# Layer 0 of an S5 + SSD + retention trunk: stages divided and reordered, and a third fp32 u tile

## Chip, cores and metric

One core of one Trainium2 chip runs the whole kernel. The metric is device time in microseconds (us) of one execution; the median of 3 runs stands for a kernel.

## What is computed

The input is x, 512 positions by 1024 features in float32; the output has the same shape. There are two layers and a final RMSNorm. Layer 0, which the change touches, is (from the reference, shortened):

```
p   = rmsnorm(x) @ w_in                       # columns: z (2048) | u (1024) | xbc (1536) | dt (16)
y_a = s5_mixer(u) * silu(z_a)                 # 64 groups of 16 channels, diagonal complex state, GELU, GLU
y_b = ssd_mixer(xbc, dt)                      # conv of 4 taps, 16 heads, 4 chunks of 128 positions
y_b = rmsnorm(y_b * silu(z_b), norm_w, 2 groups)
h   = x + concat(y_a, y_b) @ w_out
```

SSD works by chunk: a decay matrix exp(a_l - a_s) for each head times C B^T gives the part within a chunk; a state carried from chunk to chunk gives the part from before. S5 is written here as products with powers of the state matrix: the input of 8 positions is folded into one state step, the 64 steps are scanned, and the outputs are read back through the same powers. Layer 1 is a retention layer (q, k, v and gate projections, rotary, 4 chunks, 4 heads, group norm, output projection); it is not touched.

## The kernel before

Activations lie transposed in SBUF: features on partitions in tiles of 128, and 512 positions along the free side. A projection makes one 128 x 512 tile of results in one PSUM buffer. There are two forms. The unsplit form (`mm1`, line 202) is 8 fp32 matmuls on the raw weight, each of which the trace shows as two instructions. The split form (`mm3`, line 110) is 24 matmuls on parts in the fp32r type: ScalarE copies the weight to a high part and VectorE subtracts it for the low part (`split_w`, line 100), and the same is done once to the normalised x (`parts`, line 251), which gives `xh` and `xl`. `SPLIT` (line 29) names the z and u tiles that take the split form; u0, u1 and all xbc tiles take the unsplit one. u0 and u1 are run on x before it is normalised, and their results are multiplied by the norm `rbc` when they leave PSUM (line 265), because the norm is not known yet.

Layer 0 is cut into stages with one letter each (dictionary at line 477), and `ORDER` (line 36) writes out the sequence by hand:

- `x` m: one xbc tile and its convolution. `d`, `e`: step sizes and decays. `w`: split of the normalised x. `u` m, `z` m: one projection tile; u goes to DRAM and comes back in another layout, z goes to DRAM.
- `q`: S5 parameters, on VectorE, with a rotation table on GpSimd. `b` j: products O for the outputs (lines 764 to 784, GpSimd), written to DRAM. `k` j: the taps (line 786). `a` j (line 710, `s5_state`): loads U, loads `al` and `b`, makes the products `tm` and `al` from them (lines 726 to 731), runs the S matmuls on them (line 734), then the rotation and scan on VectorE. `c` j (line 802): reads O and the taps back and makes the S5 output y5.
- `s` c (line 351, `ssd`): one SSD chunk, for two head groups: transposes, state update, the decay tile `dec` (loaded from DRAM, Abs and Exp on ScalarE, mask on VectorE, lines 386 to 391), the y matmuls (lines 393 to 399) and their eviction.
- `n` gr (line 442, `ssd_norm`): gate, squares and sums on GpSimd and ScalarE, then the column sums and the root (`rstd`, line 161: matmuls `rsg..ps`, twelve small VectorE instructions, transposes `rsg..pb`), then the split into `ybh` and `ybl`. `o` m: output projection of the SSD half (`ob`), which needs all eight `ybh`/`ybl`. `p` m: S5 output times gate, and its split, which all GLU projections `gl` need.

The program text does not set the queues by itself. A scheduler runs through the program on a timeline of planned times before the run. At each step it takes, for each engine, the instruction of the highest priority whose inputs and buffers are ready on that timeline; priority is the place in the program, apart from weight loads and splits (`rank_w`, `ahead`) and evictions (`rank_e`), which are put forward. The order found so is fixed: on the chip each engine takes its instructions in that order, and so does SP, whose queue issues all transfers.

Buffers come from pools by tag (line 26): `v` has 17 slots (12 are the conv tiles), `m` 20, `p` 5, `f` 8, `s` 4, `g` (decay tiles) 3. PSUM has three tags: `acc` 3, `a` 2, `b` 3.

Of the kernel before, what the change touches and what calls it, by code (L numbers as in the profile page):

```python
# [17 lines left out]
P = 128  # L18
# [7 lines left out]
BUFS = {'x': 16, 'v': 17, 'm': 20, 's': 4, 'p': 5, 'f': 8}  # L26
POOL_P = ((1, 1), (2, 1), (3, 1))
WARM = 11
SPLIT = [f"z{m}" for m in range(16)] + [f"u{m}" for m in range(2, 8)]
SILU_Z = tuple(range(8, 16))  # L30
GELU_P = ()
AX, AZ = 200, 600
KEEP = (2, 3)
POOL_Z = (7,)
VEC_X = ((0, 0), (1, 0), (0, 1), (1, 1))
ORDER = """x8 x10 d0 x9 x11 q0 x0 x1 x2 x3 e0 b0 x4 x5 x6 x7 w0 a0 s0 u2 u3 k0 b1 s1 z0 z1 a1 c0 s2 z2 z3 u4 u5 k1 b2
 s3 z4 z5 a2 c1 z6 z7 n0 n1 u6 u7 k2 b3 a3 c2 o0 o1 z8 z9 z10 z11 k3 o2 o3 c3 z12 z13 z14 z15 o4 o5 p0 p1 p2 p3 o6 o7 p4 p5 p6 p7"""
MAGIC = 12582912.0
LOG2E = 1.4426950408889634
LN2_HI = 0.693359375  # L40
# [7 lines left out]
def trunk_kernel(ctx: ExitStack, tc: tile.TileContext, a: dict, out: bass.AP):  # L48
# [13 lines left out]
    def acc(name):  # L62
        return pp.tile([P, 512], F32, name=name, tag="acc", bufs=3)
# [122 lines left out]
    def layer0():  # L186
# [33 lines left out]
        with rank(-3000000):  # L220
            s5pr = t("m", "s5p", n=192).rearrange("p (i w) -> p i w", w=64)
            sp.dma_start(s5pr, a["s5p"])
            sp.dma_start(lnw, a["lnw"])
            w0 = []
            for k in range(KD):
                sp.dma_start(xs[k], a["xT"][k])
                if k == 0:
                    w0 += [ld_raw(a["w_u"][m], f"u{m}") for m in range(1)]
            w0 += [ld_raw(a["w_u"][m], f"u{m}") for m in range(1, 2)]
            for k in range(KD):  # L230
                q = t("p", f"xq{k}")
                act.activation(q, xs[k], AF.Square)
                act.activation(xs[k], xs[k], AF.Identity, scale=lnw[:, 0, k:k + 1])
                if k:
                    vec.tensor_tensor(sq[0], sq[0], q, op=ALU.add)
                sq.append(q)
            pu = [acc(f"u{m}") for m in range(2)]
            for k in range(KD):
                pe.matmul(pu[0], w0[0][:, k, :], xs[k], start=k == 0, stop=k == KD - 1)
            rstd(sq[:1], D, "rs0", rbc)  # L240
            mm1(pu[1], w0[1], xs)
            for k in range(KD):
                vec.tensor_tensor(xn[k], xs[k], rbc, op=ALU.mult)
        tri = const("tri", [P, P], a["tri"])
# [10 lines left out]
                xh.append(h), xl.append(lo)  # L255

        def s5_in(m):
            ps = proj(a["w_u"][m], f"u{m}") if m > 1 else pu[m]
            with rank_e():
                us = t("p", f"us{m}")  # L260
                ud, sd = us.rearrange("p (t k) -> p t k", t=T5), ps.rearrange("p (k t) -> p t k", t=T5)
                if m > 1:
                    act.activation(ud, sd, AF.Copy)
                else:
                    vec.tensor_tensor(ud, sd, rbc.rearrange("p (k t) -> p t k", t=T5), op=ALU.mult)
                sp.dma_start(u_d[:, m * P:(m + 1) * P, :].rearrange("t c k -> c t k"),
                             us.rearrange("p (t k) -> p t k", t=T5))
# [2 lines left out]
            s5.update(s5_params(s5pr))  # L270
            s5_setup(s5)

        s5_in(0)
        s5_in(1)
        sA = [P, NC4, 16]
        dtn = sv.tile(sA, F32, name="dtn")
        dda = sv.tile(sA, F32, name="dda")
# [60 lines left out]
        def conv(m):  # L338
# [8 lines left out]
            act.activation(g, g, AF.Silu)  # L347
            xbc[m] = g
        prev = [None, None]

        def ssd(c):
            yb, bT, cT = xbc[0:8], xbc[8:10], xbc[10:12]
# [13 lines left out]
            for gr in range(2):  # L366
                hs = slice(8 * gr, 8 * gr + 8)
                xdt = t("v", f"xdt{c}{gr}").rearrange("p (h d) -> p h d", d=64)
                ps_x = aux(f"px{c}{gr}", "b")
                for i in range(4):  # L370
                    pe.transpose(ps_x[:, i * P:(i + 1) * P], xbc[4 * gr + i][:, cs], ident)
                vec.tensor_tensor(xdt, ps_x.rearrange("p (h d) -> p h d", d=64),
                                  dtn[:, c, hs].unsqueeze(2).broadcast_to([P, 8, 64]), op=ALU.mult)
                if c < NC4 - 1:
                    xds = t("v", f"xds{c}{gr}")
                    vec.tensor_tensor(xds.rearrange("p (h d) -> p h d", d=64), ps_x.rearrange("p (h d) -> p h d", d=64),
                                      ds[:, c, hs].unsqueeze(2).broadcast_to([P, 8, 64]), op=ALU.mult)
                    ps_s = aux(f"st{c}{gr}", "b")
                    pe.matmul(ps_s, bn[:, gr, :], xds, start=True, stop=True)
                if c > 0:  # L380
                    ps_o = aux(f"yo{c}{gr}", "b")
                    pe.matmul(ps_o, cT[gr][:, cs], prev[gr], start=True, stop=True)
                    yo = t("v", f"yos{c}{gr}")
                    vec.tensor_tensor(yo.rearrange("p (h d) -> p h d", d=64), ps_o.rearrange("p (h d) -> p h d", d=64),  # L384
                                      ec[:, c, hs].unsqueeze(2).broadcast_to([P, 8, 64]), op=ALU.mult)
                dec = tp.tile([P, 8, P], F32, name=f"dec{c}{gr}", tag="g", bufs=3)
                sp.dma_start(dec, at_d[c, hs, :].partition_broadcast(P))
                for i in range(8):
                    act.activation(dec[:, i, :], dec[:, i, :], AF.Abs, bias=nacs[:, c, 8 * gr + i:8 * gr + i + 1])  # L389
                act.activation(dec, dec, AF.Exp, scale=-1.0)  # L390
                vec.tensor_tensor(dec, dec, cbm[:, gr, :].unsqueeze(1).broadcast_to([P, 8, P]), op=ALU.mult)
                ps_y = aux(f"y{c}{gr}", "b")
                for pr in range(4):
                    if c > 0:
                        pe.matmul(ps_y[:, pr * P:(pr + 1) * P], yo[:, pr * P:(pr + 1) * P], ident, start=True, stop=False)  # L395
                    for hh in range(2):
                        i = 2 * pr + hh
                        pe.matmul(ps_y[64 * hh:64 * hh + 64, pr * P:(pr + 1) * P], xdt[:, i, :], dec[:, i, :],
                                  start=c == 0, stop=True)
                for pr in range(4):  # L400
                    m = 4 * gr + pr
                    vec.scalar_tensor_tensor(yb[m][:, cs], xbc[m][:, cs], chp[:, 0, m:m + 1],
                                             ps_y[:, pr * P:(pr + 1) * P], op0=ALU.mult, op1=ALU.add)
                if c == 0:
                    prev[gr] = t("s", f"prev{gr}")
                    act.activation(prev[gr], ps_s, AF.Copy)
                elif c < NC4 - 1:
                    h_ = prev[gr].rearrange("p (h d) -> p h d", d=64)
                    vec.tensor_tensor(h_, h_, cd[:, c, hs].unsqueeze(2).broadcast_to([P, 8, 64]), op=ALU.mult)
                    vec.tensor_tensor(prev[gr], prev[gr], ps_s, op=ALU.add)  # L410
# [31 lines left out]
        def ssd_norm(gr):  # L442
            yb = xbc[0:8]
            sqs = []
            for i in range(4):
                m = 4 * gr + i
                zt = t("p", f"zb{m}r")
                sp.dma_start(zt, z_d[m])
                if m not in SILU_Z:
                    act.activation(zt, zt, AF.Silu)  # L450
                pool.tensor_tensor(yb[m], yb[m], zt, op=ALU.mult)
                act.activation(zt, yb[m], AF.Square)
                if i:
                    pool.tensor_tensor(sqs[0], sqs[0], zt, op=ALU.add)
                sqs.append(zt)
            rg = t("m", f"rg{gr}")
            rstd(sqs[:1], 512, f"rsg{gr}", rg)
            for i in range(4):
# [8 lines left out]
        def out_b(m):  # L467
            ps = acc(f"ob{m}")
            mm3(ps, ld_w(a["w_o0"][m, 1], f"ob{m}"), ybh, ybl)
            with rank_e():  # L470
                x = t("p", f"hb{m}")
                with after(f"ob{m}"):
# [1 line left out]
                vec.tensor_tensor(x, ps, x, op=ALU.add)  # L474
                sp.dma_start(h_d[m], x)

        stage = dict(a=lambda j: s5_state(s5, u_d, j), b=lambda j: s5_kern(s5, j), c=lambda j: s5_out(s5, j),
                     k=lambda j: s5_taps(s5, j), d=steps, e=decay, q=s5_begin, w=parts, u=s5_in,
                     s=ssd, x=conv, z=gate_in, p=glu_in, n=ssd_norm, o=out_b)
        for o in ORDER.split():  # L480
# [195 lines left out]
    def s5_setup(s5):  # L676
# [28 lines left out]
        y_d = dp.tile([8, P, SEQ], F32, name="y_d")  # L705
        o_d = dp.tile([4, 4, P, SEQ], F32, name="o_d")
        eye, dK = const("eye", [P, 16], a["eye"]), const("dK", [P, 8], a["dK"])
        s5.update(eye=eye, dK=dK, kd=kd, bd=bd, y_d=y_d, o_d=o_d, X={}, U={}, y={}, os={})

    def s5_state(s5, u_d, j):  # L710
        rot = s5["rot"]
        U = f(f"U{j}", [P, 16, NK])
        for tt in range(T5):
            sp.dma_start(U[16 * tt:16 * tt + 16],
                         u_d[tt, 256 * j:256 * j + 256, :].rearrange("(g c) k -> c g k", c=16))
        pss = [aux(f"S{j}{c}") for c in range(2)]
        for par in range(2):
            g0 = 16 * j + 8 * par
            al, b, tm = (f(f"{n}{j}{par}", [P, 2, 8, 2, 32]) for n in ("al", "b", "tm"))
# [9 lines left out]
            for c in range(2):  # L729
                eng.tensor_tensor(al[:, c], al[:, c], b[:, 1 - c], op=ALU.mult)  # L730
            eng.tensor_tensor(al[:, 1], al[:, 1], al[:, 0], op=ALU.subtract)
            for c, Pt in enumerate((tm[:, 0], al[:, 1])):
                for i in range(8):
                    pe.matmul(pss[c][64 * par:64 * par + 64, i * NK:(i + 1) * NK],  # L734
                              Pt[:, i].rearrange("p h f -> p (h f)"), U[:, 8 * par + i, :],
# [22 lines left out]
        for par, c in ((0, 0), (1, 0), (0, 1), (1, 1)):  # L758
            q = slice(64 * par, 64 * par + 64)
            eng = vec if (par, c) in VEC_X else pool  # L760
            eng.tensor_tensor(X[par][64 * c:64 * c + 64], gt[c][q], gi[c][q], op=ALU.add if c else ALU.subtract)
        s5["X"][j], s5["U"][j] = X, U

    def s5_kern(s5, j):
        pws, kd, bd = (s5[k] for k in ("pws", "kd", "bd"))
# [364 lines left out]
```

## Time and profile before

| | us |
|---|---|
| median of 3 runs | 927.87 |
| lowest, highest | 927.17, 930.09 |
| profiled execution, its own time | 926.73 |
| its span, first to last instruction | 925.0 |
| TensorE matmul (PE) busy | 874.0 |
| VectorE (DVE) busy | 549.7 |
| ScalarE (ACT) busy | 360.7 |
| GpSimd (POOL) busy | 227.3 |

Times in the trace count from the first instruction. PE's busy time includes work at the lower clock; the granted clock is given for each stretch, as a share of 2.4 GHz. PE reaches layer 1 (the first `qk` matmul) at 513 us. In a line of the timeline the brackets hold the time for which the engine stood idle before the group, and what ended it.

### The profile page before, as it was taken

To read this page: it belongs to the slowest core of one execution; us is meant where nothing else is said; L and a number is where in the kernel's file an instruction comes from. 1 tells how busy PE (TensorE), PEld (TensorE's weight loads), DVE (VectorE), ACT (ScalarE), POOL (GpSimd) and SP (SyncE) were. 2 spreads that over 40 slices of the span, in tenths; PEclk is the share of its full clock that TensorE was granted. 3 is DMA by queue.
4 is the path that set the end of the run, shared out by engine and by line. 5 is a ranking of instruction groups with operands and counts; after the bars stand their busy time and mean duration, and the time that the engine had idled before them with its cause. 6 is when DMAs were issued, how large, how long until landed. Compare 5 with 4: busy or idle time off the path is not lost.

```text
span 925.0 us, 11531 instructions
## 1 busy us (share of the span) xinstructions
PE 874.0 (94%) x4260; PEld 671.8 (73%) x4260; DVE 549.7 (59%) x986; ACT 360.7 (39%) x572; POOL 227.3 (25%) x193
## 2 busy tenths in 40 slices
PE   8797999899796699999999999999999999999996
PEld 4333457677575578788888888888888888888885
DVE  6969549867768856255444364744643544547445
ACT  4311483425334233353434325345421243254432
POOL 0089701730875380000003121301000303110020
PEclk9898999999797789999999999999999999999998
DMA  7394214775664575683543222222222222222322
GB/s 241 94 225 137 93 46 139 244 206 158 214 213 118 145 204 173 213 297 127 188 143 124 92 91 69 69 92 69 91 91 92 93 91 68 92 69 69 115 69 91
DMA packets 73623, 121.44 MB, mean 131 GB/s; under 512 B 27552, under 2 KB 38112, under 8 KB 73440
## 3 DMA queue, kind: packets, MB, share of 16 engines
q1 hardware_dynamic: 73568, 120.72, 41.3%
q8 instruction: 33, 0.54, 0.3%
q14 instruction: 22, 0.18, 0.1%
HBM read 103.61 MB, written 17.07 MB: 130 GB/s over the span
## 4 chain that ended last, share of the span: by engine, by line
PE 62%; DVE 3%; ACT 1%; DMA 1%; SPq 1%; issue 0%; ACTq 0%; DVEq 0%
PE g L114 3%; PE qk L116 3%; PE qk L115 3%; PE g L115 3%; PE g L116 3%; PE qk L114 3%; PE v L909 3%; PE v L910 3%; PE v L908 3%; PE gl L115 2%; PE gl L116 2%; PE gl L114 2%; PE ob L115 2%; PE oa L116 2%; PE out L115 1%; PE out L116 1%
## 5 line engine op out<-in xcount | busy, mean ns | idle before, releaser
L882 POOL TENSOR_TENSOR rt<-rt,ru 128x512 f32<-128x512 f32 x16 | 27.1, 1717 | 134.6 <-DVE ru L881 134.6
L951 POOL TENSOR_TENSOR os<-os,os 128x512 f32<-128x512 f32 x12 | 15.5, 1289 | 139.9 <-ACT os L949 107.0
L777 POOL TENSOR_TENSOR O<-ct,s5pws 128x512 f32<-128x512 f32 x16 | 22.1, 1384 | 109.9 <-DMA ct<-in_s5c_dram 88.4
L861 POOL TENSOR_TENSOR hs<-hs,hs 128x512 f32<-128x512 f32 x7 | 12.3, 1753 | 88.0 <-ACT hs L859 88.0
L345 DVE SCALAR_TENSOR_TENSOR cva<-xbc,cvw,cva 128x511 f32<-128x511 f32 (+2 forms) x36 | 26.7, 742 | 10.9 <-ACT cva L342 10.6
L881 DVE TENSOR_TENSOR ru<-qk,tab 128x512 f32<-128x512 f32 x16 | 11.0, 685 | 32.5 <-PE qk L116 32.5
L389 ACT ACTIVATE dec<-dec,nacs 128x128 f32<-128x128 f32 x64 | 19.6, 388 | 26.3 <-DMA dec<-at_d 26.3
L781 POOL TENSOR_TENSOR O<-O,ot 128x512 f32<-128x512 f32 x16 | 28.0, 1776 | 0.0
L777 POOL TENSOR_TENSOR ot<-ct,s5pws 128x512 f32<-128x512 f32 x16 | 22.7, 1419 | 0.0
L983 DVE TENSOR_TENSOR h<-h,out 128x512 f32<-128x512 f32 x8 | 5.5, 687 | 25.5 <-PE out L116 25.5
L1044 POOL TENSOR_TENSOR fin<-fin,fnw 128x512 f32<-128x512 f32 x4 | 5.0, 1283 | 60.4 <-ACT fq L1008 60.4
L438 POOL TENSOR_TENSOR za6r<-za6r,y 128x512 f32<-128x512 f32 x1 | 1.7, 1719 | 72.2 <-DMA h_d<-hb 72.2
L727 DVE TENSOR_TENSOR tm<-al,b 128x512 f32<-128x512 f32 x10 | 11.1, 1150 | 13.1 <-DMA b<-in_s5bP_dram 9.2
L347 ACT ACTIVATE cva<-cva 128x512 f32<-128x512 f32 x12 | 7.6, 630 | 27.9 <-DVE cva L345 25.1
L503 DVE TENSOR_TENSOR h<-oa,h 128x512 f32<-128x512 f32 x8 | 5.5, 691 | 19.6 <-PE oa L116 19.6
L509 POOL TENSOR_TENSOR s5rt<-rot,s5lv 128x512 f32<-128x512 f32 (+4 forms) x7 | 5.3, 754 | 44.6 <-DVE s5lv L663 44.4
L119 ACT ACTIVATE rh<-rt 128x512 fp32r<-128x512 f32 (+1 forms) x16 | 9.1, 577 | 16.9 <-POOL rt L882 16.9
L734 PEld LDWEIGHTS S<-U,tm 128*64 128x64 f32 x128 | 9.0, 147 | 9.2 <-issue 4.1
L824 PE MATMUL Y<-T,U 128*64 128x128 f32 x128 | 14.4, 273 | 1.3 <-DMA T<-kd 1.3
L120 DVE TENSOR_TENSOR rl<-rt,rh 128x512 fp32r<-128x512 f32 (+1 forms) x16 | 14.9, 956 | 0.6 <-ACT rh L119 0.2
L395 PE MATMUL y<-ident,yos 128*128 128x128 f32 x48 | 12.5, 346 | 2.6 <-DVE yos L384 2.6
L1039 PE MATMUL om<-wh,yh 128*128 128x512 f32 (+1 forms) x40 | 14.0, 349 | 0.5 <-DVE fin L1006 0.5
(1691 smaller groups left out, 2983.0 us busy)
## 6 DMA issues: line engine op xcount, KB each, us to landing
al<-al_d SPq DMA_DIRECT2D x64, 64.0 KB, 3.5
b<-in_s5bP_dram SPq DMA_DIRECT2D x8, 512.0 KB, 3.7
o_d<-O SPq DMA_DIRECT2D x16, 256.0 KB, 3.0
dec<-at_d SPq DMA_DIRECT2D x8, 512.0 KB, 5.2
T<-kd SPq DMA_DIRECT2D x64, 64.0 KB, 2.4
Or<-o_d SPq DMA_DIRECT2D x16, 256.0 KB, 5.5
x<-in_xT_dram SPq DMA_DIRECT2D x8, 256.0 KB, 5.0
u_d<-us SPq DMA_DIRECT2D x8, 256.0 KB, 3.1
```

The lines of the kernel that those rows point to most:

```text
L114: pe.matmul(ps, wh[:, k, :], xh[k], start=start and i == 0, stop=False)
L115: pe.matmul(ps, wh[:, k, :], xl[k], start=False, stop=False)
L116: pe.matmul(ps, wl[:, k, :], xh[k], start=False, stop=stop and i == len(ks) - 1)
L345: vec.scalar_tensor_tensor(g[:, d:], ps[:, 0:SEQ - d], cvw[:, m, j:j + 1], g[:, d:], op0=ALU.mult, op1=ALU.add)
L389: act.activation(dec[:, i, :], dec[:, i, :], AF.Abs, bias=nacs[:, c, 8 * gr + i:8 * gr + i + 1])
L777: pool.tensor_tensor(x.rearrange("p (g k c) -> p g k c", g=4, c=16), ct[:, c, par, 4 * hf:4 * hf + 4].unsqueeze(2).broadcast_to(sh), pws[: ...
L781: pool.tensor_tensor(o, o, tm, op=ALU.add)
L882: pool.tensor_tensor(t1, t1, t2, op=op)
L908: pe.matmul(ps[c], hh[kk][:, cs], wh[:, i, :], start=kk == 0, stop=False)
L909: pe.matmul(ps[c], hh[kk][:, cs], wl[:, i, :], start=False, stop=False)
L910: pe.matmul(ps[c], hl[kk][:, cs], wh[:, i, :], start=False, stop=kk == KD - 1)
L951: pool.tensor_tensor(sqs[0], sqs[0], sx, op=ALU.add)
```

## The change

1. Three u tiles instead of two take the unsplit form ahead of the norm. 2. S5's stage `a` becomes `l` (load U), `g` (load `al`, `b` and make the products) and `a` (S matmuls and scan). 3. SSD's stage `s` ends with the masked decay tile and the state update; `t` does the y matmuls and their eviction. 4. `n` ends with the sum of squares; `r` does the root, the norm and the split. 5. `ORDER` is rewritten. No instruction is added or taken away apart from the third u tile's form.

```
-SPLIT = [f"z{m}" for m in range(16)] + [f"u{m}" for m in range(2, 8)]
+SPLIT = [f"z{m}" for m in range(16)] + [f"u{m}" for m in range(3, 8)]
-ORDER = """x8 x10 d0 x9 x11 q0 x0 x1 x2 x3 e0 b0 x4 x5 x6 x7 w0 a0 s0 u2 u3 k0 b1 s1 z0 z1 a1 c0 s2 z2 z3 u4 u5 k1 b2
- s3 z4 z5 a2 c1 z6 z7 n0 n1 u6 u7 k2 b3 a3 c2 o0 o1 z8 z9 z10 z11 k3 o2 o3 c3 z12 z13 z14 z15 o4 o5 p0 p1 p2 p3 o6 o7 p4 p5 p6 p7"""
+ORDER = """x8 x10 d0 x9 x11 q0 x0 b0 x1 x2 l0 g0 x3 e0 x4 k0 x5 b1 x6 a0 x7 w0 g1 s0 u3 l1 t0 s1 z0 a1 k1 b2 z1 t1 s2 u4 c0 u5
+ t2 l2 g2 s3 z2 a2 k2 b3 z3 t3 u6 c1 u7 z4 l3 g3 z5 n0 z6 a3 z7 c2 n1 z8 k3 r0 z9 z10 r1 c3 z11 o0 p0 p1 o1 z12 p2 z13 p3 o2 z14
+ p4 p5 z15 o3 p6 p7 o4 o5 o6 o7"""
...
-            w0 += [ld_raw(a["w_u"][m], f"u{m}") for m in range(1, 2)]
+            w0 += [ld_raw(a["w_u"][m], f"u{m}") for m in range(1, 3)]
-            pu = [acc(f"u{m}") for m in range(2)]
+            pu = [acc(f"u{m}") if m < 2 else aux(f"u{m}", "b") for m in range(3)]
...
             mm1(pu[1], w0[1], xs)
+            mm1(pu[2], w0[2], xs)
...
-                if m > 1:
+                if m > 2:
                     act.activation(ud, sd, AF.Copy)
...
                 vec.tensor_tensor(dec, dec, cbm[:, gr, :].unsqueeze(1).broadcast_to([P, 8, P]), op=ALU.mult)
+                held[c, gr] = xdt, dec, yo if c > 0 else None
+                if c == 0:
+                    prev[gr] = t("s", f"prev{gr}")
+                    act.activation(prev[gr], ps_s, AF.Copy)
...
+        def ssd_y(c):
+            yb, cs = xbc[0:8], slice(c * P, (c + 1) * P)
+            for gr in range(2):
+                xdt, dec, yo = held[c, gr]
                 ps_y = aux(f"y{c}{gr}", "b")
...
                 sqs.append(zt)
+            held["sq", gr] = sqs
+
+        def ssd_parts(gr):
+            yb, sqs = xbc[0:8], held["sq", gr]
             rg = t("m", f"rg{gr}")
             rstd(sqs[:1], 512, f"rsg{gr}", rg)
...
+    def s5_load(s5, u_d, j):
         U = f(f"U{j}", [P, 16, NK])
...
+    def s5_state(s5, j):
+        s5["P"][j] = []
...
-            for c, Pt in enumerate((tm[:, 0], al[:, 1])):
+            s5["P"][j].append((tm[:, 0], al[:, 1]))
+
+    def s5_scan(s5, j):
+        rot, U = s5["rot"], s5["U"][j]
+        pss = [aux(f"S{j}{c}") for c in range(2)]
+        for par in range(2):
+            for c, Pt in enumerate(s5["P"][j][par]):
```

## Rows read from the trace of the kernel before

**Rows 1.** The page: the span, and each engine's busy time.
```profile
span 925.0 us, 11531 instructions
...
PE 874.0 (94%) x4260; PEld 671.8 (73%) x4260; DVE 549.7 (59%) x986; ACT 360.7 (39%) x572; POOL 227.3 (25%) x193
```

**Rows 2.** Busy time by stretch of the span (the header names the columns).
```profile
core 0: us, PE busy (x) PEld busy (x) DVE busy (x) ACT busy (x) POOL busy (x), PEclk, DMA share, GB/s
23.00:39.50 16.50, 11.32 (x24) 4.78 (x23) 16.50 (x67) 4.41 (x8) 0.00 (x0) 0.79 0.34 96
74.00:98.00 24.00, 18.36 (x38) 7.80 (x37) 23.06 (x32) 5.43 (x8) 23.16 (x26) 0.86 0.26 87
...
172.00:186.00 14.00, 10.22 (x57) 7.28 (x56) 12.53 (x13) 4.93 (x11) 6.28 (x4) 0.88 0.90 294
186.00:240.00 54.00, 54.00 (x364) 40.92 (x363) 32.80 (x54) 24.03 (x49) 13.27 (x11) 1.00 0.65 189
240.00:260.00 20.00, 14.95 (x79) 10.85 (x78) 18.47 (x19) 2.20 (x4) 20.00 (x12) 0.66 0.62 190
260.00:288.00 28.00, 28.00 (x218) 22.23 (x217) 21.48 (x27) 13.77 (x23) 18.62 (x14) 1.00 0.55 182
288.00:332.00 44.00, 26.83 (x144) 21.21 (x143) 33.24 (x57) 14.65 (x24) 22.48 (x16) 0.69 0.50 132
```

**Rows 3.** Timeline of PE to 98 us (start, length, instruction, idle before).
```profile
22.07 1.88 PE L204 MATMUL u<-x,u1w 128*128 128x512 f32 x4
26.92 0.62 PE L171 MATMUL rs0pb<-ident,rs0y 128*128 128x128 f32 x4 [2.97 <-DVE rs0y L158]
29.75 9.90 PE L204 MATMUL xbc<-xn,xbc8w 128*128 128x512 f32 x16 [2.21 <-DVE xn L243]
39.48 7.03 PE L204 MATMUL xbc<-xn,xbc10w 128*128 128x512 f32 x16
...
87.79 9.88 PE L204 MATMUL xbc<-xn,xbc2w 128*128 128x512 f32 x16 [3.43 <-issue]
```

**Rows 4.** Timeline of PE from 170 to 330 us: its longest waits.
```profile
177.18 0.50 PE L116 MATMUL z<-xh,z3l 128*128 128x512 f32 x1 [3.78 <-DVE z3l L107]
...
243.49 1.51 PE L734 MATMUL S<-U,tm 128*64 128x64 f32 x12 [2.42 <-DVE tm L728]
247.64 0.80 PE L395 MATMUL y<-ident,yos 128*128 128x128 f32 x2 [2.64 <-DVE yos L384]
...
295.03 1.84 PE L165 MATMUL rsg0ps<-ones,zb0r 128*128 128x1 f32 x8 [6.16 <-POOL zb4r L454]
299.39 0.87 PE L171 MATMUL rsg0pb<-ident,rsg0y 128*128 128x128 f32 x3 [2.53 <-DVE rsg0y L158]
...
314.47 1.12 PE L734 MATMUL S<-U,tm 128*64 128x64 f32 x16 [1.28 <-ACT ks L796]
...
320.92 1.94 PE L734 MATMUL S<-U,al 128*64 128x64 f32 x16 [3.84 <-DVE al L731]
```

**Rows 5.** Timeline: split u2's first matmul, u3's first; u results times rbc; u2's low part.
```profile
138.43 0.48 PE L114 MATMUL u<-xh,u2h 128*128 128x512 f32 x1
...
143.98 0.39 PE L114 MATMUL u<-xh,u3h 128*128 128x512 f32 x1
...
33.83 2.05 DVE L265 TENSOR_TENSOR us<-u,rbc 128x512 f32<-128x512 f32 x2
...
L107 DVE TENSOR_TENSOR u2l<-u2w,u2h x1: 1224/1224/1224, 118.2 to 118.2; 128x1024 fp32r<-128x1024 f32 x1
```

**Rows 6.** Instructions of line 107, min/median/max ns, and group of z7l in 240 to 332 us.
```profile
L107 DVE TENSOR_TENSOR z11l<-z11w,z11h x1: 1225/1225/1225, 345.2 to 345.2; 128x1024 fp32r<-128x1024 f32 x1
...
L107 DVE TENSOR_TENSOR z7l<-z7w,z7h 128x1024 fp32r<-128x1024 f32 x1 | 2.1, 2115 | 0.0
```

**Rows 7.** Timeline: SP's al loads, DVE's wait at a product; ACT's wait for decay loads.
```profile
57.15 3.19 SPq L722 DMA_DIRECT2D al<-al_d  x6
...
66.17 2.55 DVE L727 TENSOR_TENSOR tm<-al,b 128x512 f32<-128x512 f32 x2 [7.22 <-DMA b<-in_s5bP_dram]
...
ACT dec L389 <- DMA dec<-at_d: 26.3, 6, 7.9
```

More of the change, by code (lines that the diff above doesn't have):

```diff
@@ L257, in s5_in @@
         def s5_in(m):
-            ps = proj(a["w_u"][m], f"u{m}") if m > 1 else pu[m]
+            ps = proj(a["w_u"][m], f"u{m}") if m > 2 else pu[m]
             with rank_e():
@@ L271, in s5_begin @@
             s5_setup(s5)
-        s5_in(0)
-        s5_in(1)
+        for m in range(3):
+            s5_in(m)
         sA = [P, NC4, 16]
@@ L349, in layer0 @@
         prev = [None, None]
+        held = {}
         def ssd(c):
@@ L391, in ssd @@
                 vec.tensor_tensor(dec, dec, cbm[:, gr, :].unsqueeze(1).broadcast_to([P, 8, P]), op=ALU.mult)
+                held[c, gr] = xdt, dec, yo if c > 0 else None
+                if c == 0:
+                    prev[gr] = t("s", f"prev{gr}")
+                    act.activation(prev[gr], ps_s, AF.Copy)
+                elif c < NC4 - 1:
+                    h_ = prev[gr].rearrange("p (h d) -> p h d", d=64)
+                    vec.tensor_tensor(h_, h_, cd[:, c, hs].unsqueeze(2).broadcast_to([P, 8, 64]), op=ALU.mult)
+                    vec.tensor_tensor(prev[gr], prev[gr], ps_s, op=ALU.add)
+        def ssd_y(c):
+            yb, cs = xbc[0:8], slice(c * P, (c + 1) * P)
+            for gr in range(2):
+                xdt, dec, yo = held[c, gr]
                 ps_y = aux(f"y{c}{gr}", "b")
@@ L403, in ssd @@
                                              ps_y[:, pr * P:(pr + 1) * P], op0=ALU.mult, op1=ALU.add)
[L404 to L410, printed above, removed]
         z_d = dp.tile([16, P, SEQ], F32, name="z_d")
@@ L475, in out_b @@
                 sp.dma_start(h_d[m], x)
-        stage = dict(a=lambda j: s5_state(s5, u_d, j), b=lambda j: s5_kern(s5, j), c=lambda j: s5_out(s5, j),
+        stage = dict(l=lambda j: s5_load(s5, u_d, j), g=lambda j: s5_state(s5, j), a=lambda j: s5_scan(s5, j), t=ssd_y, r=ssd_parts, b=lambda j: s5_kern(s5, j), c=lambda j: s5_out(s5, j),
                      k=lambda j: s5_taps(s5, j), d=steps, e=decay, q=s5_begin, w=parts, u=s5_in,
@@ L707, in s5_setup @@
         eye, dK = const("eye", [P, 16], a["eye"]), const("dK", [P, 8], a["dK"])
-        s5.update(eye=eye, dK=dK, kd=kd, bd=bd, y_d=y_d, o_d=o_d, X={}, U={}, y={}, os={})
-    def s5_state(s5, u_d, j):
-        rot = s5["rot"]
+        s5.update(eye=eye, dK=dK, kd=kd, bd=bd, y_d=y_d, o_d=o_d, X={}, U={}, y={}, os={}, P={})
+    def s5_load(s5, u_d, j):
         U = f(f"U{j}", [P, 16, NK])
@@ L715, in s5_state @@
                          u_d[tt, 256 * j:256 * j + 256, :].rearrange("(g c) k -> c g k", c=16))
-        pss = [aux(f"S{j}{c}") for c in range(2)]
+        s5["U"][j] = U
+    def s5_state(s5, j):
+        s5["P"][j] = []
         for par in range(2):
@@ L761, in s5_state @@
             eng.tensor_tensor(X[par][64 * c:64 * c + 64], gt[c][q], gi[c][q], op=ALU.add if c else ALU.subtract)
-        s5["X"][j], s5["U"][j] = X, U
+        s5["X"][j] = X
     def s5_kern(s5, j):
```

## The prediction

> **What bounds the kernel now.** I read the page first, then the busy time stretch by stretch, then TensorE's timeline for its waits, then the instructions that the waits name. The page says that TensorE (PE) is busy in 874.0 of 925.0 us [rows 1], so nothing but PE work and PE waits can set the end. The stretches show where the 51 us without work lie. From 186 to 240 us and from 260 to 288 us PE is busy throughout at a granted clock of 1.00 [rows 2]. The losses sit in five places, all in layer 0: A 23 to 39.5, B 74 to 98, C 172 to 186, D 240 to 260, E 288 to 332 us. In each the granted clock is also below 1.00 (0.66 in D, 0.69 in E), that is, for a part of it PE ran at 1.2 instead of 2.4 GHz after it had waited. The reader is to see that a wait is paid twice: as idle time and as slow work behind it.
>
> What a stretch loses is bounded from its row. Idle time is its length less PE busy. Slow clock costs at most (1 - clock) x length, when all of the slow time fell on work, and half of the idle time less than that, when PE idled only at the slow clock. D: 20.00 - 14.95 = 5.05 idle, 0.34 x 20 = 6.8. E: 44.00 - 26.83 = 17.17 idle, 0.31 x 44 = 13.6. D and E together: 22.2 idle, 20.4 clock, so a loss of 31.5 to 42.7, middle 37 us, or 1.67 us for each us of idle. C: 3.8 idle + 1.7 clock = 5.5 at most.
>
> Who ends the waits: in A the norm chain on VectorE (DVE) [rows 3]; in D and E the S5 products (S waits for tm and al, 2.42 and 3.84), the S matmul behind ks 1.28, the group norm (rsg0ps waits 6.16 for GpSimd's (POOL's) zb4r, rsg0pb 2.53 for DVE), and y behind yos 2.64 [rows 4]. Each waiting instruction is the head of PE's queue, and projections stand behind it.
>
> **The third unsplit u tile.** u2 becomes 16 fp32 matmuls on the unnormalised x, issued while the norm is computed. u0 and u1 end at 23.95 (22.07 + 1.88); then PE waits 2.97 and 2.21, and xbc8's 16 matmuls take 9.90 at the slow clock where xbc10's take 7.03 [rows 3]. With u2, 7.03 long, xbc8 starts near 31.0 and, if the clock holds, ends near 38.0 instead of 39.5: the tile costs nothing, because the norm chain hides it. Without that cover it would cost 7.03. Its later form, 24 split matmuls from 138.43 to 143.98, disappears: -5.5 us [rows 5]. The 1.5 us won at 38 I drop: at 77 to 88 us PE waits for DVE's work anyway (B, DVE busy 23.06 of 24.00 [rows 2]), and DVE gets 1.0 more there (us for u2 with rbc, 2.05 for two) against 1.2 less later (u2l) [rows 5]. So A and B give -5.5, with bounds of -7.0 (kept) and 0 (the hole shrinks and the DVE backlog grows by as much). u2's 512 KB weight now goes ahead of xbc8's on SP's queue; xbc8 is needed only at 31 us.
>
> **The S5 products apart.** Loads of U (8 transfers), then al and b with the products (18 transfers), now come stages ahead of the S matmuls: g0 ahead of x3 and a0 after x6; between g1, g2, g3 and their a there is at least one projection and an SSD or norm stage. Instructions and bytes are the same. SP issues six al loads in 3.19 us [rows 7], so 26 of them hold its queue 13.8 us, ahead of weights for xbc3 and later, which PE reaches from 97.7 (87.79 + 9.88 [rows 3]). DVE once stood 7.22 us at such a product because b had not landed, with conv work queued behind it [rows 7]; that is half of B's cause. Moving g0 earlier could shrink this wait or lengthen it; I take zero, bounds -7 to +7. On POOL the O products b1 to b3 come a little earlier, ahead of the group norm's multiplications instead of partly behind; I price that in the new waits. In D and E the S waits, 2.42 + 1.28 + 3.84, should go, since a projection of 5.5 us or more is queued in their place; what is late next is the scan on DVE, which PE meets only at the Y matmuls.
>
> **The norm's root apart.** n0 and n1 only multiply, square and add; the column sums, the root and the split come as r0 and r1, with two or more projections or S5 stages between. The 6.16 and 2.53 go. Late next: o0 needs all eight ybh and ybl, with c3 and z11 as cover.
>
> Sum for D and E: 7.5 + 8.7 = 16.2 of 22.2 idle us, 0.73 of a loss of 31.5 to 42.7, is 23 to 31; I take the middle, -27. C stays: z3l is late on DVE, 3.78 us [rows 4], and no edit reaches that.
>
> **The SSD outputs apart.** s_c ends with the decay tile and the state update; t_c, with two projections between (one at t0), runs y. xdt and yos of both head groups are held till then (four of the five free v slots beside the 12 conv tiles), and two of the three decay buffers. The trace does not show this. At best it removes the yos wait (2.64, 4.4 with its clock share). At worst the decay loads, for which ScalarE (ACT) now waits 26.3 us out of PE's sight [rows 7], reach PE: 26.3 x 1.67 = 44. I take two new waits of the size of yos's, 2 x 2.64 x 1.67 = +8.8, nearer to the row that PE showed than to ACT's.
>
> **Sum:** -5.5 - 27 + 8.8 = -23.7. The profiled execution took 926.73 us (span 925.0), which is 1.1 below the median of 927.87. 926.7 - 23.7 + 1.1 = **904 us**.
>
> **Rivals.** *DVE takes over.* In the quiet a weight split took DVE 1.22 us (z11l), beside POOL 2.12 (z7l) [rows 6]; in 240 to 332 us DVE is busy 73.2 of 92. If the products and y stay late because DVE is full, only the rsg waits go: 8.69 of 22.2, 14.5 us, less the 8.8: 926.7 - 5.5 - 5.7 + 1.1 = 917. For it: D, where DVE is busy 18.47 of 20. Against: 260 to 288, where DVE is busy 77% with POOL at 66% and PE never waits. The Trainium skill (SBUF — State Buffer, SBUF: two separate sides) says that a DVE instruction with two SBUF inputs and a GpSimd one lock each other out for the whole instruction. By that rule packing the same DVE and POOL work into less time gains nothing from overlap; z7l against z11l agrees with it.
>
> *All waits go.* C, D and E wholly (5.5 + 37) and 7.0 in A: 926.7 - 49.5 + 1.1 = 878. Against: PE's order is fixed before the run, DVE's times vary by the factor above.
>
> *The edit hardly changes the queue.* The scheduler lets ready work pass work that isn't, so u6 and u7, written after n0, already run before it. If the emitted order stays, only u2 counts: 926.7 - 5.5 + 1.1 = 922.
>
> *Slower: the decay tiles.* t_c gives the decay buffers and v slots back late, so the next chunk's load starts late, its Abs, Exp and mask end late, and PE stands at y of t1 to t3 with projections queued behind. The chain then delays n and r, so their waits stay. Gains 5.5 + (7.54 / 22.2) x 37 = 18; cost 26.3 x 1.67 = 44 in full, 22 if half reaches PE: 932 to 954, I say 943. It decides once 0.41 of the 26.3 reach PE. Against: each t has two projections (11 us) as cover, and y waited on DVE, never on a transfer. The Trainium skill (Perfetto Trace Analysis, Optimization Strategy) reads a repeating gap on the engine that should be full as possibly too few buffers; no gap at y repeats in this trace yet.
>
> **Chances.** Forecast 904: 0.42. DVE takes over 917: 0.22. All waits go 878: 0.07. Queue unchanged 922: 0.08. Slower 943: 0.21. Within 0.3% (2.8 us, about what a measurement can tell from no change) fall 0.03 of the fourth and 0.02 of the last. So faster 0.76, same 0.05, slower 0.19. The range runs from 880 (all but the last of the waits) to 938 (the lower half of the slow case); above it lies about 0.12, below about 0.06. The forecast's own range is 890 to 914, by the loss bounds and by none to twice the new waits.
>
> **What would show it.** Right: PE goes from u0/u1 into u2 without a wait and xbc8 takes about 7 us; no wait of PE on zb4r, tm or al; the granted clock of the 90 us ahead of the first ob near 0.95; layer 1, untouched, of the same length. Wrong: PE waits at y with dec behind it; DVE waits for b or al while conv is queued; POOL's O products standing ahead of the norm's multiplications; or ob and gl waiting for ybl and y5l after the last z has been used up as filler.

## The result and the profile after

The changed kernel takes 932.74 us (median of 20 runs, 927.74 to 937.63); the kernel before, run beside it, 927.25 (20 runs, 924.59 to 931.70). The ratio is 1.0054 [1.0036, 1.0072]: slower by 0.5%, where 904 had been forecast. The profiled execution took 927.74 us, the fastest of the 20, so its rows show about 5 us less than the median.

The page of the kernel after, in the part that answers to [rows 1]:

```profile
span 925.9 us, 11510 instructions
...
PE 876.2 (95%) x4252; PEld 670.6 (72%) x4252; DVE 553.2 (60%) x986; ACT 357.8 (39%) x569; POOL 226.2 (24%) x193
```

PE is busy 2.2 us longer than before; the third tile alone takes 7.03 us in its unsplit form (16 matmuls) where its split form took 5.5 (24). Where the time went is seen in six stretches of layer 0, first of the kernel before, then of the kernel after (columns as in [rows 2]):

```profile
0.00:100.00 100.00, 85.64 (x206) 37.76 (x207) 83.39 (x276) 30.32 (x49) 50.89 (x76) 0.93 0.56 161
100.00:160.00 60.00, 60.00 (x292) 36.77 (x291) 38.11 (x60) 36.49 (x67) 10.87 (x11) 1.00 0.32 103
160.00:230.00 70.00, 66.22 (x446) 50.05 (x445) 52.37 (x77) 29.70 (x58) 26.67 (x18) 0.98 0.67 200
230.00:300.00 70.00, 56.26 (x351) 43.60 (x351) 51.84 (x63) 28.19 (x47) 49.63 (x32) 0.84 0.59 182
300.00:390.00 90.00, 79.42 (x496) 62.71 (x496) 50.38 (x70) 27.34 (x40) 27.62 (x18) 0.90 0.60 179
390.00:480.00 90.00, 90.00 (x419) 74.59 (x416) 42.77 (x52) 39.37 (x53) 1.72 (x1) 1.00 0.56 194
```

```profile
0.00:100.00 100.00, 81.53 (x199) 35.67 (x200) 92.16 (x267) 27.46 (x44) 60.58 (x82) 0.95 0.62 179
100.00:160.00 60.00, 57.00 (x240) 30.04 (x239) 38.29 (x58) 33.37 (x59) 25.58 (x22) 0.96 0.29 95
160.00:230.00 70.00, 65.98 (x422) 50.61 (x421) 52.42 (x77) 24.46 (x50) 18.51 (x12) 0.89 0.69 191
230.00:300.00 70.00, 64.65 (x432) 48.28 (x431) 48.19 (x70) 26.28 (x47) 28.80 (x18) 0.95 0.61 167
300.00:390.00 90.00, 79.59 (x505) 64.52 (x504) 53.58 (x84) 46.10 (x74) 30.66 (x20) 0.92 0.64 203
390.00:480.00 90.00, 90.00 (x399) 74.33 (x398) 36.80 (x44) 29.61 (x37) 2.04 (x1) 1.00 0.51 173
```

From 230 to 300 us, where the S5 and norm waits stood, PE gained 8.4 us of work (64.65 for 56.26) and clock (0.95 for 0.84). The first 160 us lost nearly as much, 4.1 and 3.0 us of work, and from 160 to 230 us the clock fell from 0.98 to 0.89. Layer 1 kept its length (411.7 us from the first `qk` matmul to the end in both), so everything was decided here; the output tile ob4 starts at 404.8 us, before at 403.9.

The start, which answers to [rows 3] (timeline of PE in the kernel after):

```profile
13.25 4.46 PE L205 MATMUL u<-x,u2w 128*128 128x512 f32 x10
17.54 1.02 PE L240 MATMUL u<-x,u0w 128*128 128x512 f32 x2
18.40 1.02 PE L205 MATMUL u<-x,u2w 128*128 128x512 f32 x2
...
24.41 0.95 PE L166 MATMUL rs0ps<-ones,xq 128*128 128x1 f32 x8
...
33.13 0.62 PE L172 MATMUL rs0pb<-ident,rs0y 128*128 128x128 f32 x4 [2.52 <-DVE s5scr L665]
35.37 8.82 PE L205 MATMUL xbc<-xn,xbc8w 128*128 128x512 f32 x16 [1.62 <-DVE xn L245]
...
71.98 3.75 PE L205 MATMUL xbc<-xn,xbc11w 128*128 128x512 f32 x4 [6.89 <-issue]
...
99.52 8.80 PE L205 MATMUL xbc<-xn,xbc2w 128*128 128x512 f32 x16 [4.12 <-issue]
```

Twelve of u2's sixteen matmuls (4.46 + 1.02 us) stand ahead of the norm's column sums rs0ps, which start at 24.41 instead of 19.46: u2 has u1's old place, and eight of u1's matmuls and the last four of u0's now stand ahead of rs0ps as well. The waits behind them, 2.52 and 1.62, are still there, and xbc8 starts at 35.37 instead of 29.75. The tile went in front of the hole and moved it. By xbc2 the delay is 11.7 us (99.52 against 87.79). The 6.89 at xbc11 has no releaser in the profile; by time it ends when VectorE's convolution L347 does (71.88), behind work on the S5 parameters.

The sums of squares that rs0ps reads were not late. VectorE's last addition (timeline of DVE, kernel after) ends at 14.27, in the kernel before at 14.47:

```profile
13.58 0.69 DVE L236 TENSOR_TENSOR xq<-xq,xq 128x512 f32<-128x512 f32 x1
```

So rs0ps stood 10 us behind other matmuls in PE's fixed order, and 5 us in the kernel before. No run puts it ahead of u1 too.

The longest waits after that, which answer to [rows 4] (timeline of PE, kernel after):

```profile
157.13 0.50 PE L116 MATMUL u<-xl,u3h 128*128 128x512 f32 x1 [2.32 <-DVE xl L121]
...
213.46 0.80 PE L411 MATMUL y<-ident,yos 128*128 128x128 f32 x2 [4.01 <-DVE yos L387]
...
278.72 0.66 PE L844 MATMUL Y<-Or,X 128*64 128x128 f32 x2 [5.35 <-DMA Or<-o_d]
...
339.33 1.05 PE L166 MATMUL rsg0ps<-ones,zb0r 128*128 128x1 f32 x8
345.04 1.09 PE L172 MATMUL rsg0pb<-ident,rsg0y 128*128 128x128 f32 x4 [4.65 <-DVE rsg0y L159]
```

The S waits and the 6.16 us on zb4r are gone. New are xl 2.32, Or 5.35 and later 2.30; yos grew from 2.64 to 4.01 and rsg0pb from 2.53 to 4.65.

### The profile page after: what moved, and what is told of

Read it like the earlier page. It is cut to its first block, busy times and chain, and to the rows that moved or that the text cites. A ratio compares the mean times of both kernels' runs of the same rounds, so it can differ in the third digit from the quotient of the medians.

```text
span 925.9 us, 11510 instructions
## 1 busy us (share of the span) xinstructions
PE 876.2 (95%) x4252; PEld 670.6 (72%) x4252; DVE 553.2 (60%) x986; ACT 357.8 (39%) x569; POOL 226.2 (24%) x193
## 4 chain that ended last, share of the span: by engine, by line
PE 76%; DVE 7%; DMA 6%; ACT 4%; issue 3%; SPq 2%; POOL 2%; ACTq 0%; POOLq 0%
PE xbc L205 7%; PE g L115 3%; PE qk L117 3%; PE g L116 3%; PE qk L116 3%; PE g L117 3%; PE qk L115 3%; PE v L930 3%; PE v L931 3%; PE v L929 3%; PE z L117 2%; PE z L115 2%; PE z L116 2%; PE gl L115 2%; PE gl L116 2%
## 5 line engine op out<-in xcount | busy, mean ns | idle before, releaser
L347 DVE SCALAR_TENSOR_TENSOR cva<-xbc,cvw,cva 128x511 f32<-128x511 f32 (+2 forms) x36 | 26.7, 741 | 12.3 <-ACT cva L344 11.9
L392 ACT ACTIVATE dec<-dec,nacs 128x128 f32<-128x128 f32 x64 | 19.4, 389 | 16.6 <-DMA dec<-at_d 16.6
L802 POOL TENSOR_TENSOR O<-O,ot 128x512 f32<-128x512 f32 x16 | 21.6, 1379 | 0.0
L844 PE MATMUL Y<-Or,X 128*64 128x128 f32 x64 | 13.6, 297 | 8.1 <-DMA Or<-o_d 8.1
L845 PE MATMUL Y<-T,U 128*64 128x128 f32 x128 | 16.7, 290 | 0.0
L487 DVE TENSOR_TENSOR hb<-ob,hb 128x512 f32<-128x512 f32 x8 | 5.5, 690 | 17.8 <-PE ob L117 17.8
L205 PE MATMUL xbc<-xn,xbc11w 128*128 128x512 f32 x16 | 9.2, 727 | 6.9 <-issue 6.9
L120 ACT ACTIVATE rh<-rt 128x512 fp32r<-128x512 f32 (+1 forms) x16 | 9.1, 577 | 16.9 <-POOL rt L903 16.9
L411 PEld LDWEIGHTS y<-ident,yos 128*128 128x128 f32 x48 | 8.1, 209 | 9.2 <-issue 4.5
```

The lines of the kernel that those rows point to most:

```text
L205: pe.matmul(ps, raw[:, k, :], x[k], start=k == 0, stop=k == KD - 1)
L347: vec.scalar_tensor_tensor(g[:, d:], ps[:, 0:SEQ - d], cvw[:, m, j:j + 1], g[:, d:], op0=ALU.mult, op1=ALU.add)
L802: pool.tensor_tensor(o, o, tm, op=ALU.add)
```

## The experiments

Each median is compared with runs of the kernel before on the same chip; in brackets is the 95% interval of the ratio.

| run | edit | us | ratio to before, 95% |
|---|---|---|---|
| e1 | third u tile alone, old sequence | 949.63 | 1.0234 [1.0195, 1.0273] |
| e2 | change, u2 left split | 934.40 | 1.0082 [1.0052, 1.0111] |
| e3 | stages divided, old sequence, u2 split | 926.48 | 0.9993 [0.9975, 1.0012] |
| e4 | change, u2 behind the column sums | 917.48 | 0.9896 [0.9863, 0.9930] |
| e5 | before, u2 as in e4 | 926.99 | 1.0004 [0.9976, 1.0032] |
| e6 | e4, w0 ahead of a0 | 912.20 | 0.9847 [0.9822, 0.9872] |
| e7 | e4, c1 ahead of k2 and b3 | 914.77 | 0.9873 [0.9842, 0.9903] |
| e8 | e4, r0 and r1 earlier | 920.59 | 0.9929 [0.9901, 0.9956] |
| e9 | e6, norm root in PSUM tag b | 910.55 | 0.9840 [0.9808, 0.9871] |
| e10 | e9, c1 first | 913.70 | 0.9871 [0.9842, 0.9899] |
| e11 | e6, t joined to s | 914.32 | 0.9874 [0.9852, 0.9897] |
| e12 | e6, l and g joined to a | 922.35 | 0.9959 [0.9940, 0.9977] |
| e13 | e2, w0 ahead of a0 | 931.80 | 1.0068 [1.0042, 1.0094] |
| e14 | e9, z written from ScalarE's queue | 909.91 | 0.9826 [0.9801, 0.9851] |

**The change in its parts: e1, e2, e3.** e1 puts the third tile into the kernel before, e2 takes it out of the change, e3 divides the stages but leaves the parts together.

```
 e1:-SPLIT = ... for m in range(2, 8)]    +SPLIT = ... for m in range(3, 8)]  (and u2 out of ORDER)
 e2:-... range(3, 8)]                     +... range(2, 8)]      ORDER: s0 u2 u3 l1 t0
 e3: ORDER = "... w0 l0 g0 a0 s0 t0 u2 u3 k0 b1 s1 t1 z0 z1 l1 g1 a1 c0 ... n0 r0 n1 r1 u6 u7 ..."
```

> Only the third unsplit u tile, in the kernel before. Theory E (the early part loses: u2's matmuls stand ahead of the norm's column sums, so everything behind the norm starts 5 to 6 us later, and the split u2's 5.5 us that go are eaten by that): 926 to 931 us, rs0ps at about 24.4 us instead of 19.5, xbc8 at about 35 instead of 29.75. Theory L (the early part gains the 5.5 of the prediction, the late part loses it again in new waits): about 922 us.

> The change without the third unsplit u tile (u2 split, just ahead of u3). Theory E: 5 us or more faster than the change, 922 to 928 us, with rs0ps back at 19.5 us. Theory L: 5 us slower than the change, about 938 us, since a gain is taken away and the new waits stay.

> The stages divided as in the change, but each part right behind the other in the old sequence, and u2 split as before. If dividing alone costs nothing, 925 to 930 us, as before. If the held tiles or the moved state update cost something by themselves, 932 us or more, with PE waiting at y behind dec.

Dividing costs nothing (926.48). The tile in the old sequence costs 22.4 us, the sequence without it 7.2; the two together cost 5.5. So they are not terms that add. Both theories missed e1 (949.63) and e2 (934.40). Theory E's signs came (rs0ps at 24.54 and xbc8 at 35.50 in e1, rs0ps at 19.19 in e2), but its times left out that xbc2 would start 15.8 us late in e1 (103.62), and that the new sequence loses by itself.

**The tile behind the column sums: e4, e5.** u2's matmuls with the first four feature tiles are queued behind rs0ps, the other four behind rs0pb, and u2's weight is loaded after u1's. The two parts of the edit have no runs of their own.

```
+                sums[name] = pe.matmul(ps[:, c:c + 1], ...).ins
...
+            w0 += [ld_raw(a["w_u"][m], f"u{m}", ahead=-8 * (m - 1)) for m in range(1, 3)]
...
-            mm1(pu[2], w0[2], xs)
+            for k in range(KD):
+                with tc.issue_after(sums["rs0"] if k < 4 else sums["rs0b"]):
+                    pe.matmul(pu[2], w0[2][:, k, :], xs[k], start=k == 0, stop=k == KD - 1)
```

> The change with u2's matmuls queued behind the norm's column sums, the last four behind the norm's transposes, and u2's weight loaded behind u1's. Theory E: rs0ps at about 19.5 us, xbc8 from 31 to 32 us at full clock, and 6 to 11 us faster than the change: 922 to 927 us. Theory L: as the change, within 3 us (930 to 936), since the lead is lost at the next wait on VectorE.

> The kernel before (old sequence, undivided stages) with the third unsplit u tile queued behind the norm's sums, as in e4. If the tile is worth the prediction's 5.5 us once it stands behind the norm, 920 to 923 us, and the new sequence is then worth 3 to 6 us more (e4 has 917.5). If the new sequence brings nothing, this run is at 915 to 919 us; if the tile helps only together with the new sequence, at 926 us or more.

Timeline of PE in e4, the same stretch as above:

```profile
18.90 0.95 PE L168 MATMUL rs0ps<-ones,xq 128*128 128x1 f32 x8
...
23.23 3.60 PE L247 MATMUL u<-x,u2w 128*128 128x512 f32 x8
26.66 0.60 PE L174 MATMUL rs0pb<-ident,rs0y 128*128 128x128 f32 x4
27.10 3.60 PE L247 MATMUL u<-x,u2w 128*128 128x512 f32 x8
30.53 7.03 PE L207 MATMUL xbc<-xn,xbc8w 128*128 128x512 f32 x16
...
86.12 4.56 PE L207 MATMUL xbc<-xn,xbc2w 128*128 128x512 f32 x5 [6.29 <-issue]
```

This is the picture of the prediction: both waits are gone, and xbc8 runs from 30.5 to 37.6 at 7.03. In the new sequence that is worth 15.3 us (932.74 to 917.48), in the old one 22.6 (949.63 to 926.99); the 15.3 is more than theory E's 6 to 11. But in the old sequence the tile so placed gains nothing over the split form: what it saves is waited for later (from 60 us on PE waits 40.1 us in e5, 34.5 before; timeline of PE in e5: xbc2 for 6.68 us, where [rows 3] show 3.43, then a low part of a weight and one of y):

```profile
86.49 3.74 PE L206 MATMUL xbc<-xn,xbc2w 128*128 128x512 f32 x4 [6.68 <-issue]
...
244.26 0.80 PE L116 MATMUL z<-xh,z7l 128*128 128x512 f32 x1 [5.34 <-DVE z7l L107]
...
324.68 0.80 PE L115 MATMUL ob<-ybl,ob0h 128*128 128x512 f32 x1 [7.28 <-DVE ybl L120]
```

**The new waits of the sequence: e6, e7, e8.** Each moves one stage in e4's sequence.

```
 e6:-b1 x6 a0 x7 w0 g1           +b1 x6 x7 w0 a0 g1
 e7:-a2 k2 b3 z3 t3 u6 c1 u7     +a2 c1 k2 b3 z3 t3 u6 u7
 e8:-n1 z8 k3 r0 z9 z10 r1 c3    +r0 n1 z8 r1 z9 k3 z10 c3
```

> e4 with the split of the normalised x (w0) ahead of the first S5 scan (a0) instead of behind it. If the scan's VectorE work holds up xl, PE's waits on xl and z0l near 145 us (2.8 us in e4) go and the time falls by 3 to 8 us, to 910 to 914. If VectorE is full there whatever comes first, 916 to 919.

> e4 with the S5 output stage c1 ahead of the taps k2 and the products b3. If SP's queue is what holds c1's loads of O (they stand behind the write of k2's taps, which waits for VectorE), PE's wait on Or near 264 us (5.6 us) goes and the time falls by 6 to 10 us, to 908 to 912. If the loads are late for lack of slots, the wait stays and so does the time, within 3 us.

> e4 with r0 right behind c2 and r1 right behind z8, so that z8 to z11 and c3 stand between the roots and o0. If the norm chain costs because the projections meant as its cover were used up ahead of it, PE's waits on rsg0pb, ybh and ybl (4.3 us) go and the time falls by 5 to 10 us, to 908 to 913. If the sums of squares on GpSimd come no earlier, PE waits for zb0r or zb4r instead and the time stays or rises.

With w0 first the waits on xl and z0l (1.92 and 0.83 in e4) are gone and 5.3 us with them. With c1 first the Or wait at 264 us is gone, but the time is only 2.7 us lower, which the intervals do not tell apart from e4, and not the 6 to 10 expected; another Or wait, at 347 us, is 4.93 (e4: 1.24).

What held Or at 264 us? SP's own waits in e4 between 236 and 268 us show two things: the write of the taps ks waits for DVE ahead of the Or loads, and one of the Or loads (L832) waits for DVE itself.

```profile
SPq L825 <- DVE ks L823: 13.8, 1, 13.8
SPq L832 <- DVE mg L786: 6.9, 1, 6.9
```

The second ends last (timelines of SP, DVE and PE in e4):

```profile
252.05 1.86 SPq L832 DMA_DIRECT2D Or<-o_d  x2
...
260.22 0.69 DVE L786 TENSOR_TENSOR mg<-X,gi 64x512 f32<-64x512 f32 x1
260.94 0.32 SPq L832 DMA_DIRECT2D Or<-o_d  x1
...
264.02 0.66 PE L848 MATMUL Y<-Or,X 128*64 128x128 f32 x2 [5.59 <-DMA Or<-o_d]
```

Once ks is written, two loads go out by 253.9; the third follows only when DVE has ended a step of a2's scan (260.91), lands 3.0 us later, and PE starts. In the program Or takes its tiles from tag m, as the scan's gi, X and mg do, so this load waits for a buffer. The rival of e7, lack of slots, is thus not refuted but borne out for this wait: with c1 ahead of k2 and b3 its loads also come to their buffers earlier, and e7 cannot tell the two causes apart. The kernel after shows the same ahead of its 5.35 (SP waits 7.0 us for DVE's mg).

e8 missed: rsg0ps stayed at 327.9 us (e4: 328.6), and the time rose by 3.1, within the intervals. The place in the program was not what held the norm's column sums.

**What holds the norm's root: e9, e10.** In the kernel after, POOL's last sum for the first group and the column sums that use it are 20 us apart (timeline of POOL; PE's lines stand above):

```profile
316.89 2.27 POOL L463 TENSOR_TENSOR zb0r<-zb0r,zb3r 128x512 f32<-128x512 f32 x1
```

It ends at 319.16; rsg0ps runs at 339.33, directly ahead of rsg0pb, which then waits 4.65 us for the twelve small DVE instructions. The root's PSUM buffers have tag a, two buffers that the S, K, Y and Yt results use too; e9 gives them tag b.

```
-    def rstd(sqs, n, name, bc):
-        ps = aux(name + "ps")
+    def rstd(sqs, n, name, bc, tag="a"):
+        ps = aux(name + "ps", tag)
...
-            rstd(sqs[:1], 512, f"rsg{gr}", rg)
+            rstd(sqs[:1], 512, f"rsg{gr}", rg, "b")
```

> e6 with the group norm's column sums and transposes in the PSUM tag b (three buffers, free once the SSD stages are done) instead of a (two buffers, which the S, K and Y stages hold). If r0 stood late in PE's queue because the scheduler had no buffer of tag a for it, its sums now come tens of matmuls earlier with projections between sums, transposes and ob: PE's waits on rsg0pb, ybh and ybl (6.2 us in e6) and the slow clock behind them go, and the time falls by 6 to 12 us from 912.2, to 900 to 906. If the sums on GpSimd were the reason, PE waits for zb0r instead and the time stays within 3 us.

> e9 with c1 ahead of k2 and b3 as in e7: the sum of what helped. If the effects add, 2 to 3 us below e9 (e7 gained 2.7 on e4), 898 to 904; if the wait only moves to the next stage on SP's queue, as e9 within 3 us.

Timeline of PE in e9:

```profile
298.25 0.95 PE L168 MATMUL rsg0ps<-ones,zb0r 128*128 128x1 f32 x8
...
312.98 0.65 PE L174 MATMUL rsg0pb<-ident,rsg0y 128*128 128x128 f32 x4 [1.98 <-DVE rsg0y L159]
...
331.56 0.40 PE L848 MATMUL Y<-Or,X 128*64 128x128 f32 x2 [4.63 <-DMA Or<-o_d]
```

The buffer was what held it: POOL's last sum ends at 295.78 in e6 and 295.99 in e9, and the column sums run at 319.95 and 298.25; work stands between them and rsg0pb, and the next waits at `ob` shrink from 0.72 and 0.78 in e6 to 0.41. The time fell by 1.65 us only, less than the intervals can tell apart (0.6 by the ratios): at Or PE waits 4.63 where e6 has 2.74, and at yos 6.53 (195 us) where e6 has 3.25. e10 missed too: c1 first is 3.2 us above e9, as little told apart as the gain in e7; the Or waits stayed (3.00, 1.96, 1.16), and al made PE wait 3.88.

**What the two other divisions are worth: e11, e12.** Both join parts again in e6's sequence.

```
 e11:-s0 u3 l1 t0 s1 z0 a1 k1 b2 z1 t1    +s0 t0 u3 l1 s1 t1 z0 a1 k1 b2 z1   (t2, t3 likewise)
 e12:-x2 l0 g0 x3 ... w0 a0 g1            +x2 x3 ... w0 l0 g0 a0              (1 to 3 likewise)
```

> e6 with each t right behind its s, so that the SSD outputs are no longer apart. If keeping them apart gives y its cover, PE waits more at yos and the time rises by 3 us or more, to 915 or above. If the held xdt, yos and decay tiles cost as much as the cover gives, within 3 us of 912.2; if they cost more, below 909.

> e6 with l and g right ahead of their a, so that the S5 products are no longer apart. If moving them ahead removes PE's waits at the S matmuls, those waits (7.5 us in the kernel before) come back and the time rises by 5 us or more, to 917 or above. If the scheduler pulls the products forward by itself, within 3 us of 912.2.

The S5 products apart are worth 10.1 us. Joined, PE's waits at the S matmuls are 9.6 us in all; e6 keeps 4.7, of which 2.51 behind ScalarE's y and 1.9 without a named releaser. Two of those in e12 (timeline of PE):

```profile
184.63 0.90 PE L759 MATMUL S<-U,tm 128*64 128x64 f32 x6 [2.80 <-POOL tm L747]
...
320.62 1.63 PE L759 MATMUL S<-U,al 128*64 128x64 f32 x16 [4.18 <-POOL al L750]
```

The SSD outputs apart are worth 2.1 us, with overlapping intervals: the wait on yos is 3.62 joined and 3.25 apart. No run joins r to n again, so the third division has no price of its own.

**What stayed open, tried once more: e13, e14.** e13 asks whether xl behind a0's scan is why the sequence without the tile loses; e14 whether SP's queue is why Or is late in e9.

```
 e13 (in e2):-b1 x6 a0 x7 w0 g1               +b1 x6 x7 w0 a0 g1
 e14 (in e9):-sp.dma_start(z_d[m], zt)        +act.dma_start(z_d[m], zt)
```

> The change with u2 kept in its split form (934.40) and w0, the split of the normalised x, moved ahead of a0's scan. Theory: without the third tile the new sequence loses because u2's split matmuls, the first to need xl, stand at 144.5 and 147.4 us for 3.26 and 1.85 us while DVE does a0's scan, and the wait costs 1.67 us for each us. With w0 first these waits go: 934.4 - 8.5 = 926, no slower than before (within 2). Rival: the xl waits are paid for elsewhere (st behind xds 5.81 at 201 us, Or 2.40), the sequence itself is the worse one: 931 or more.

> The best version so far (910.55) with the z results written to DRAM from ScalarE's own queue instead of SyncE's; TensorE's and VectorE's instructions stay in the same order. Theory: the Or loads come late (PE waits 4.63, 1.02 and 1.23 us at 331 to 344) because they stand on SyncE's queue behind a z write that waits 7.1 us for ScalarE; on ScalarE's queue that write holds up no loads, the Or waits fall below 2 us and the time to 905 to 908. Rival: Or is late because its buffers or the bus are, or the next write in the queue (ks, also from ScalarE) takes the wait over: Or waits within 1 us of before, time within 2 us of 910.5.

In e13 the xl waits are gone, but the time fell by 2.6 us, within the intervals: the rival holds. Against e6, from which it differs by the tile alone, z1 ends at 178.5 us instead of 166.0: the split tile's 5.7 us, and waits of 0.79, 0.78 and 2.31 us at 148 to 156 on DVE and ScalarE work. The other 7 us are spread over waits of 1.3 to 3.9 and have no single cause that these runs show. In e14 the next write in SP's queue took the wait over (SP's own waits, 296 to 346 us; first e9, then e14), Or fell only from 4.63 to 3.03, and the time stayed:

```profile
SPq L431 <- ACT ks L821: 7.1, 1, 7.1
```

```profile
SPq L825 <- DVE ks L823: 6.2, 1, 6.2
```

## Why the prediction was wrong, step by step

**The step that failed: "the tile costs nothing, because the norm chain hides it".** That held only if u2 stood behind rs0ps and rs0pb. The prediction took this order from "issued while the norm is computed" and did not ask where the scheduler would put matmuls that need x alone. They went first, though on the chip the sums of squares were ready at 14.27, 1 us after u2's first matmul (why the planned times had it otherwise, no run shows), and the norm, from which all conv tiles hang, came 5 us later. The step priced the tile's place at -7.0 to 0; put in front, the tile measured +15.3 against the place that was assumed (e4). With u2 in that place the rest of the forecast's direction holds: 917.5, and 912.2 with w0 moved.

**B as a buffer for A.** The step said that 1.5 us more or less at 38 us is lost at 77 to 88 anyway, since PE waits for DVE there (the profile names ScalarE's dtt for the 2.21 us at 77, itself behind DVE, and nothing for the 3.43 at 88). A lead is indeed lost: xbc8 ends 2 us earlier in e4 than before, and xbc2 waits 6.29 instead of 3.43. A delay is not absorbed: 5.6 us at xbc8 became 11.7 at xbc2, with DVE busy 92.16 of the first 100 us (before 83.39).

**The tile's later form, -5.5.** Right as a count, but no term that adds: well placed it gave 0 in the old sequence (e5) and 17 to 20 in the new (e2 to e4; e13 to e6).

**The S5 products apart** was right: no S wait is left in the kernel after, and in e6's sequence the division is worth 10.1 us (e12). The DVE wait for b, 7.22 in [rows 7], which was taken at zero with both signs, is gone as well.

**The norm's root apart.** Half right. The 6.16 went, but rsg0pb's 2.53 became 4.65 and the clock fell behind it. Sums and root ran back to back, since the sums found no PSUM buffer until 339 us (e9 shows this in e6's sequence). In the rival "the edit hardly changes the queue" the prediction named this for the whole change; it was true of this one edit. The buffer (e9) brought 1.65 us, within the intervals.

So the sum of -27 for D and E was too large: -10.1 is what the S5 products showed singly, and the root has no such figure. All stages together, priced at -27 + 8.8 = -18.2, measured +7.2 without the tile (e2), -9.5 with the tile well placed (e5 to e4) and -16.9 with it badly placed (e1 to the change). The size of this term failed as well, and since the effects do not add, no split of the miss between tile and stages is shown. What was late next was named wrongly for the norm: not o0's parts (0.72 and 0.78), but the Or loads, a wait that the prediction did not have. It had put the scan on DVE next, which PE would meet at the Y matmuls. PE met it there, but through the buffers that the scan holds (5.35), and later behind a write on SP's queue (e9).

**The SSD outputs apart** was priced at +8.8 and measured -2.1 (e11, within the intervals). ACT's wait for decay loads, 26.3 in [rows 7], fell to 16.6, and PE never waited for dec: the slower rival's mechanism did not occur (waits of ACT, kernel after):

```profile
ACT dec L392 <- DMA dec<-at_d: 16.6, 3, 9.8
```

**The rivals.** "DVE takes over" came nearest in kind: xl, yos and xbc11 wait for DVE. None had the cause that decided, a delay of the norm by the very tile that was to fill its wait. The sign "PE goes from u0/u1 into u2 without a wait" was fulfilled and said nothing; "xbc8 takes about 7 us", with its start at 31, was the one that could fail, and it failed: 8.82 us from 35.37. The signs for D and E came (no wait on zb4r, tm or al, a clock of 0.93 from 258 to 348 us, layer 1 of the same length) in a kernel that was slower all the same.

## What to carry to other kernels

Filler for a wait must be ready, and it must stand behind the work that starts the wait: where a scheduler takes what is ready first on planned times, work without inputs to wait for can go ahead of the chain and delay it, so pin it there (15 to 23 us here), and compare in the trace when the chain's inputs were ready with when it ran. A stage that is divided gains only if its first half also finds a buffer at its new place; look at tags that it shares. After each wait that is removed read the transfer queue: a write whose data is late holds every load behind it (e9), and a load can itself wait for its buffer (e4). The effects of single edits need not add (22.4 and 7.2 came to 5.5).

## What was not expected of the hardware

In e4 one write of the taps waited 13.8 us on SP's queue for its data, with the loads of a stage that has no part in it behind it; PE's 5.59 us ended with the load that then waited 6.9 more for its buffer. In e9 a z write waited 7.1 us, the Or loads went out right behind it (328.60), and PE waited 4.63 for them. And the idle time of PE does not fix what the clock costs (stretches of 20 us, first the kernel after, then e9):

```profile
340.00:360.00 20.00, 12.65 (x44) 9.87 (x43) 10.87 (x37) 5.91 (x10) 0.00 (x0) 0.66 0.63 181
```

```profile
320.00:340.00 20.00, 13.59 (x81) 9.52 (x79) 16.60 (x35) 11.44 (x19) 0.00 (x0) 0.83 0.59 187
```

With 7.35 us idle the granted clock was 0.66, with 6.41 it was 0.83. The prediction's 1.67 us for each idle us is a mean over one part of one kernel, and waits were priced with it that cost less (in e13 8.5 us were expected, 2.6 measured).

The fastest version, e14 (909.91 us, with e9 at 910.55 not told apart from it), beats the kernel before by 1.7% and the change by 2.3% (from the ratios).
